# The pooling mixer's input product as sixteen pairs of seven products, its results through memory

## Chip, cores and metric

The kernel runs on one core of a Trainium2 chip. The metric is the device time of one execution in microseconds, taken as the median of several runs. The engines are named as in the profile: PE (matrix products; PEld loads its weights), DVE (elementwise, reads SBUF and the matmul results in PSUM), ACT (elementwise with a function table), POOL or Pool (elementwise, SBUF alone), SP (its queue issues all DMAs here).

## What is computed

Two transformer-like blocks over 1024 positions and 1024 channels. The first has a mixer (input product, a short and a long convolution, output product) and a gated FFN. The second begins with the pooling layer that the change is about, and ends with an attention layer:

```python
def pool_mixer(h, w_in, w_group, scale, w_out):
    u, z = jnp.split(h @ w_in, 2, axis=-1)            # 1024 -> 2 x 2048
    p = causal_multiscale_pool(u).reshape(B, S, 4, 512)
    y = jnp.einsum('bsgc,gcd->bsgd', p, w_group).reshape(B, S, 2048) * scale
    return (y * jax.nn.silu(z)) @ w_out               # 2048 -> 1024
# h = modulate(rmsnorm(x)); x = x + gate * pool_mixer(h, ...)
# pool: trailing mean over 2, 4, 8 or 16 positions (by channel group) minus u
```

The FFN of the first block is silu(conv3(h @ w_gate)) * (h @ w_up), then @ w_down. The shift, scale and gate vectors of the second block come from products of a small vector with large matrices, done on DVE.

## The kernel before

Activations lie with channels on the partitions: a tile is 128 channels by 512 positions, and positions come in two chunks, c = 0 and 1. Every fp32 operand is split in two parts, `hi` (rounded by ACT) and `lo` (the rest, a subtraction on Pool or DVE), and a product is three matmuls: hi.hi, hi.lo, lo.hi. Results are in eight PSUM banks.

The program is written in the order in which it is issued; each engine runs its own instructions in that order. Two devices interleave work: `chains`, generators of which `pump()` runs every one a step further, so that a number of `yield`s sets how many steps lie between its parts (`WAIT`, L30), and `bg`, a queue of small background jobs of which `pump(n)` runs n. Weights come in by `tick` (L245), which counts matmuls and starts DMAs and splits a fixed count ahead of their use.

An input product goes column by column: `mm_col` (L294) does 24 matmuls for 128 output channels and one chunk. For the FFN this is replaced by a Strassen-like scheme with seven products for eight: the two chunks and the two halves of the input channels are the blocks of the activations, a pair of 128-column units the blocks of the weights. `blocks_of_h` (L743) makes the activations' blocks, 11 and 21 of chunk 0 and then t2, t3, t4, t1, 22 of differences with chunk 1; class `Pair` (L819) makes the sums of weights s1 to s4 (`sums` L845, `added` L840), splits them (`keep` L832), runs a product of 12 matmuls (`product` L871, matmuls L882) and takes results from PSUM (`evac` L887). `steps` (L129) is the order: products 1 and 2 of the first six pairs, which need chunk 0 alone, then the rest of the first four, and from there on two pairs at a time, 14 products. `SUMS_AT` makes the first four pairs' sums on DVE in steps 1 to 4. Up to step 11 only chunk 0's blocks are needed; meanwhile `chain_ffn` (L795) makes chunk 1's norm and blocks. The FFN's results are stored to memory (`ff`) and loaded back for w_down.

The pooling layer before (L1345 on) uses `mm_col`: for each of four channel groups, four u units of two chunks, pooled by DVE (`pool_p` L1290: doublings of the window, L1298), interleaved with z units (`do_z`), the group product (`do_gm` L1323, matmuls L1333) and the output product of the units that are ready (`down`, matmuls L311). Its entry follows `chunk_out`, the last rows of w_down chunk by chunk: `evac_last_ffn` (L1211) adds into x and makes two sums of squares, `chain_pool` (L1246) makes the norm: column sums on DVE (`block_sums` L334), a small matmul (L347), a power on Pool (L389), a diagonal on DVE and ACT (`diag` L367), a spread by PE (L382, L383). u's first four units run over chunk 0 while chunk 1's norm is made. x is rescaled in bg (L1268).

## Time and profile before

| | us |
|---|---|
| median of 3 runs (2081.71 to 2082.65) | 2081.8 |
| the profiled execution | 2080.15 |
| its span, first to last instruction | 2078.4 |
| PE busy | 1995.9 |
| DVE busy | 1337.7 |
| POOL busy | 964.2 |
| ACT busy | 804.5 |

By the first matmuls of each part, the FFN's products run from 339.4 to about 801 us of the span, w_down to about 1053, the pooling layer's products from 1053.5 to about 1641, then attention. How to read the views: the timeline lists an engine's instructions with their start, duration, line of the code, and in brackets how long the engine sat idle before one and whose end released it. A matmul's duration in the timeline counts its overlap with the one before, so the distance of two starts is its price. Windows give each engine's busy time in a stretch, and PEclk, the share of PE's full clock that was granted. The chain of waits is followed back from the last instruction to what released each one.

### The profile page before, as it was taken

Reading aid. Unit: us, or ns where it says so; the run is one execution under the profiler, and the core shown is the slowest. Engines: PE = TensorE matmul, PEld = TensorE weight load, DVE = VectorE, ACT = ScalarE, POOL = GpSimd, SP = SyncE. Lnnn points to the kernel's source line nnn. Section 1 sums busy time; section 2 is a strip of 40 time slices with the busy share of each in tenths; the row PEclk is TensorE's granted clock in tenths of the full one; section 3 lists DMA queues with packets and bytes.
Section 4 is the critical chain, followed back from the end, with each engine's and each line's share of the span. In section 5 each row is a group of like instructions: output and inputs, shape, how many; then the busy total and the mean of one; then the engine's idle time right before and its main releaser. Section 6 shows DMA issues by size and latency. Waiting matters only on the chain.

```text
span 2078.4 us, 25796 instructions
## 1 busy us (share of the span) xinstructions
PE 1995.9 (96%) x9112; PEld 1655.3 (80%) x9112; DVE 1337.7 (64%) x2199; ACT 804.5 (39%) x1583; POOL 964.2 (46%) x816
## 2 busy tenths in 40 slices
...
GB/s 209 51 61 41 117 98 59 1 102 163 152 173 194 172 196 325 197 73 100 11 52 31 61 41 41 61 41 51 61 41 56 36 122 60 58 56 32 112 1 81
DMA packets 95969, 186.64 MB, mean 90 GB/s; under 512 B 10928, under 2 KB 17504, under 8 KB 95840
## 3 DMA queue, kind: packets, MB, share of 16 engines
...
## 4 chain that ended last, share of the span: by engine, by line
PE 80%; DVE 12%; issue 2%; DMA 2%; ACT 2%; POOL 1%; SPq 1%; DVEq 0%; ACTq 0%; POOLq 0%
PE p L302 34%; PE p L311 20%; PE p L882 15%; PE p L1333 4%; PE p L1827 2%; PE o L1632 1%; PE pT L1605 1%; DVE ws L842 1%; DVE cps L528 1%; DMA fl<-ff 1%; DVE c L916 1%; DMA adaw<-in_kv_ada_w 1%; DVE hu L1229 1%; PE sc L1552 1%; PE sc L1551 1%
## 5 line engine op out<-in xcount | busy, mean ns | idle before, releaser
L196 POOL TENSOR_TENSOR wlo<-raw,whi 128x512 fp32r<-128x512 f32 x260 | 350.3, 1368 | 327.2 <-ACT whi L195 157.5
L311 PE MATMUL p<-alo,whi 128*128 128x512 f32 x784 | 308.4, 393 | 7.0 <-POOL alo L421 7.0
L302 PE MATMUL p<-hhi,whi 128*128 128x512 f32 x784 | 308.5, 393 | 6.7 <-ACT hhi L414 6.7
L302 PE MATMUL p<-hlo,whi 128*128 128x512 f32 x784 | 307.7, 392 | 3.5 <-DVE hlo L415 3.5
L311 PE MATMUL p<-ahi,whi 128*128 128x512 f32 x784 | 309.1, 394 | 0.7 <-ACT yo L708 0.7
L311 PE MATMUL p<-ahi,wlo 128*128 128x512 f32 x784 | 308.0, 393 | 0.0
L302 PE MATMUL p<-hhi,wlo 128*128 128x512 f32 x784 | 307.1, 392 | 0.0
L882 PE MATMUL p<-hhi,whi 128*128 128x512 f32 x616 | 244.9, 398 | 15.5 <-DVE q L894 8.0
L882 PE MATMUL p<-hlo,whi 128*128 128x512 f32 x616 | 243.6, 395 | 0.0
L882 PE MATMUL p<-hhi,wlo 128*128 128x512 f32 x616 | 243.1, 395 | 0.4 <-POOL wlo L837 0.4
L195 ACT CAST whi<-raw 128x512 fp32r<-128x512 f32 x260 | 150.4, 618 | 239.9 <-PE p L311 149.1
L311 PEld LDWEIGHTS p<-alo,whi 128*128 128x128 f32 x784 | 149.1, 190 | 39.1 <-POOL alo L421 8.3
L302 PEld LDWEIGHTS p<-hhi,whi 128*128 128x128 f32 x784 | 148.7, 190 | 36.4 <-ACT hhi L414 6.7
L302 PEld LDWEIGHTS p<-hlo,whi 128*128 128x128 f32 x784 | 148.6, 190 | 34.8 <-DVE hlo L415 4.9
L311 PEld LDWEIGHTS p<-ahi,whi 128*128 128x128 f32 x784 | 148.9, 190 | 32.0 <-ACT yo L708 1.1
L311 PEld LDWEIGHTS p<-ahi,wlo 128*128 128x128 f32 x784 | 149.0, 190 | 31.4
L302 PEld LDWEIGHTS p<-hhi,wlo 128*128 128x128 f32 x784 | 148.3, 189 | 31.3 <-DVE wlo L196 0.2
L1343 DVE SCALAR_TENSOR_TENSOR x<-p,modv,x 128x512 f32<-128x512 f32 x128 | 95.7, 750 | 119.9 <-PE p L311 119.5
L528 DVE SCALAR_TENSOR_TENSOR cps<-u,vec,cps 128x1024 f32<-128x1024 f32 (+1 forms) x140 | 150.6, 1075 | 4.5
L882 PEld LDWEIGHTS p<-hhi,whi 128*128 128x128 f32 x616 | 117.9, 191 | 41.5 <-ACT c L914 8.4
L837 POOL TENSOR_TENSOR wlo<-ws,whi 128x512 fp32r<-128x512 f32 x66 | 96.7, 1471 | 92.7 <-ACT whi L834 80.2
L882 PEld LDWEIGHTS p<-hhi,wlo 128*128 128x128 f32 x616 | 118.0, 192 | 26.1 <-POOL wlo L837 0.8
...
## 6 DMA issues: line engine op xcount, KB each, us to landing
...
raw<-in_a_w_in SPq DMA_DIRECT2D x64, 256.0 KB, 3.0
raw<-in_w_gate SPq DMA_DIRECT2D x44, 256.0 KB, 5.0
raw<-in_w_up SPq DMA_DIRECT2D x44, 256.0 KB, 5.1
ff<-f SPq DMA_DIRECT2D x44, 256.0 KB, 4.8
raw<-in_w_down SPq DMA_DIRECT2D x44, 256.0 KB, 4.8
fl<-ff SPq DMA_DIRECT2D x44, 256.0 KB, 5.4
raw<-in_w_in SPq DMA_DIRECT2D x40, 256.0 KB, 3.1
```

The source lines that it names most:

```text
L195: (DVE.tensor_copy if on_dve else ACT.copy)(hi, t)
L196: (DVE if on_dve else POOL).tensor_tensor(lo, t, r32(hi), ALU.subtract)
L302: PE.matmul(ps, lhsT=wt[k // 4][:, sl], rhs=hh[k, c], start=(n == 0), stop=(n == 23))
L311: PE.matmul(ps, lhsT=wt[d // 4][:, sl], rhs=hh[c], start=(n == 0), stop=(n == last))
L528: DVE.scalar_tensor_tensor(dst[:, lo:hi], u[:, lo + k:hi + k], V("conv_b_w", k * 4 + j), src[:, lo:hi], ALU.mult, ALU.add)
L837: eng.tensor_tensor(lo, x, r32(hi), ALU.subtract)
L842: DVE.tensor_tensor(t, x, y, op)
L882: PE.matmul(ps, lhsT=wt[:, sl], rhs=hh, start=(begins and n == 0), stop=(n == 11), skip_group_check=True)
L916: bg.append(lambda k=k: DVE.scalar_tensor_tensor(y[:, 0:T], g[:, k:k + T], w(k), y[:, 0:T], ALU.mult, ALU.add))
L1333: PE.matmul(ps, lhsT=wt[k // 2][:, o:o + 128], rhs=hx[k, c], start=(n == 0), stop=(n == 11))
L1343: DVE.scalar_tensor_tensor(X[d, c], ps, modv[:, goff + d:goff + d + 1], X[d, c], ALU.mult, ALU.add)
L1827: PE.matmul(ps, lhsT=wt[d // 4][:, sl], rhs=hh[c][:, lo:hi], start=(n == 0), stop=(n == 11))
```

## The change

The pooling layer's input product takes the FFN's scheme. `plan` makes the order for any list of pairs; the FFN's is now gate and up pairs in turn, the pooling layer's sixteen pairs alternate u and z units (four groups' units in order). Class `Products` holds what was the FFN's loop. In both stages the first two pairs' sums of weights are made by DVE in the second chunk's rows of the product before (`lead`, one half of `sums` for each of four rows), and the next two pairs' by Pool in steps 1 and 3; in the first 12 steps every weight's low part is Pool's. `blocks_of_h` gets the shift vector, makes each operand a step before ACT casts it and issues DVE's low part a step later still.

In the pooling layer x is stored to `xp`, the pooled units to `pp` and silu(z) to `zz`, and they are loaded back: x and group 0 in the last ten steps, the other groups during the output product. The group product and the output product follow as a stage of their own. The diagonal of the second norm of each chunk (`d1`) is made after the blocks, and x is rescaled during the first group product. The taps of the FFN's convolution enter `bg` one after the other. The modulation's small matmul comes six yields after its sums instead of two. w_down's groups are 4, 4, 4, 4, 2, 4 units instead of 2, 4, 4, 4, 4, 4; its loads are cut two a step, and half of x is loaded later. The core of the diff:

```diff
-        "ffn0": (2, 1, 1), "ffn1": (4, 1, 2), "pool0": (2, 0, 1), "pool1": (4, 0, 2),
+        "ffn0": (2, 1, 1), "ffn1": (4, 1, 2), "pool0": (2, 1, 1), "pool1": (5, 2, 2),
...
+LEAD = (2, 4, 5, 6, 6, 6, 7, 8)
...
-    blocks = [[("w_gate", 0), ("w_gate", 2)], [("w_up", 0), ("w_gate", 4)]]
-    blocks += [[("w_up", f), ("w_gate", f + 4)] for f in range(2, NF - 4, 2)]
-    blocks.append([("w_up", NF - 4), ("w_up", NF - 2)])
-    pairs = [g for b in blocks for g in b]
...
+    def plan(pairs):
+        steps = [(g, 1) for g in pairs[:SIDE]] + [(g, 2) for g in pairs[:SIDE]]
+        steps += [(g, p) for p in (1, 2) for g in pairs[SIDE:EARLY]]
+
+        sums_at = {1: pairs[2], 3: pairs[3]}
+        steps += [(g, p) for p in (6, 7, 4, 5, 3) for g in pairs[:SIDE]]
+        for n in range(SIDE, len(pairs), 2):
+            for p in (1, 6, 2, 7, 5, 4, 3):
+                if n < EARLY and p in (1, 2):
+                    continue
+                steps += [(g, p) for g in pairs[n:n + 2]]
+        use = {}
+        for n, ((name, f), p) in enumerate(steps):
+            for u in ((f,) if p in (1, 2) else (f, f + 1)):
+                use.setdefault((name, u), 12 * n)
+        for n, (name, f) in [(0, g) for g in pairs[:2]] + list(sums_at.items()):
+            use[name, f + 1] = 12 * n
+        for name, f in sorted(use, key=lambda k: use[k]):
+            col(name, f)
+            stage_mm[name] = 12 * len(steps)
+        first_use.update(use)
+        return pairs, steps, sums_at
...
+    FFN = plan([(n, f) for f in range(0, NF, 2) for n in ("w_gate", "w_up")])
+    DOWN = ((0, 1, 2, 3), (4, 5, 6, 7), (8, 9, 10, 11), (12, 13, 14, 15), (16, 17), (18, 19, 20, 21))
...
+    POOLED = plan([("a_w_in_2", e) for f in range(0, 16, 2) for e in (f, 16 + f)])
...
+        queue = []
+
+        def cut(name, i, x, sh=None, on_pool=None):
+            hi = S("hhi", F32R)
+            if sh is None:
+                ACT.copy(hi, x)
+            elif on_pool:
+                y = S("hs")
+                ACT.activation(y, x, ACTF.Identity, bias=sh)
+                x, sh = y, None
+                ACT.copy(hi, x)
+            else:
+                ACT.activation(hi, x, ACTF.Identity, bias=sh)
+            if on_pool:
+                put_block(name, i, hi, x, sh, True)
+            else:
+                queue.append(lambda: put_block(name, i, hi, x, sh))
...
+        def later_on():
+            for _ in range(len(queue)):
+                queue.pop(0)()
+
+        sh = [shift and shift(k) for k in range(NK)]
         if c == 0:
             for k in range(NK):
                 hf[k] = get(k)
-                low("11" if k < 4 else "21", k % 4, hf[k], high(hf[k]), True)
+                later_on()
+                cut("11" if k < 4 else "21", k % 4, hf[k], sh[k], shift is None or k % 2)
                 if k % 2:
                     yield
+            later_on()
...
+        for name, make, shs in (("t2", make_t2, sh[4:]), ("t3", make_t3, d3), ("t4", make_t4, [None] * 4),
+                                ("t1", lambda i: t1[i], [None] * 4), ("22", lambda i: h2[i], sh[4:])):
             for i in range(4):
-                cut(name, i, ts[i])
+                t = make(i)
+                later_on()
                 yield
-        while due:
-            low(*due.pop())
+                cut(name, i, t, shs[i], i % 2)
+                yield
...
-            eng = DVE if small_op["n"] % 7 in SUB_DVE else POOL
+            eng = DVE if not small_op["early"] and small_op["n"] % 7 in SUB_DVE else POOL
...
-        def sums(self):
-            self.s1 = self.added(self.half(1, 0), self.half(1, 1), ALU.add)
-            self.s2 = self.added(self.s1, self.half(0, 0), ALU.subtract)
-            self.s3 = self.added(self.half(0, 0), self.half(1, 0), ALU.subtract)
-            self.s4 = self.added(self.half(0, 1), self.s2, ALU.subtract)
+        def sums(self, eng, n):
+            if n in (None, 0):
+                self.s1 = self.added(self.half(1, 0), self.half(1, 1), ALU.add, eng)
+                self.s2 = self.added(self.s1, self.half(0, 0), ALU.subtract, eng)
+            if n in (None, 1):
+                self.s3 = self.added(self.half(0, 0), self.half(1, 0), ALU.subtract, eng)
+                self.s4 = self.added(self.half(0, 1), self.s2, ALU.subtract, eng)
...
-        bg.append(lambda: ACT.activation(y[:, 0:T], g[:, 0:T], ACTF.Copy, scale=w(0)))
-        for k in (1, 2):
-            bg.append(lambda k=k: DVE.scalar_tensor_tensor(y[:, 0:T], g[:, k:k + T], w(k), y[:, 0:T],
-                                                           ALU.mult, ALU.add))
+
+        def scale():
+            ACT.activation(y[:, 0:T], g[:, 0:T], ACTF.Copy, scale=w(0))
+            for k in (1, 2):
+                bg.append(lambda k=k: tap(k))
+
+        def tap(k):
+            DVE.scalar_tensor_tensor(y[:, 0:T], g[:, k:k + T], w(k), y[:, 0:T], ALU.mult, ALU.add)
+            if k == 2:
+                bg.append(last)
...
+        def lead(self, d):
+
+            small_op["early"] = True
+            if d < 4:
+                self.group[self.pairs[d // 2]].sums(DVE, d % 2)
+            self.prep_to(LEAD[d])
+
+        def run(self, hook):
+            dma_ahead = clock["dma"]
+            clock["dma"] = FFN_DMA
+            for n, (g, p) in enumerate(self.steps):
+                self.prep_to(n + PREP_AHEAD + 1)
+                if n in self.sums_at:
+                    self.group[self.sums_at[n]].sums(POOL, None)
+                if n == 2 * EARLY:
+                    small_op["early"] = False
+                while len(stores) > 1:
+                    stores.popleft()()
+                self.group[g].product(p)
+                pump(2 if len(bg) > 4 else 1)
+                self.group[g].evac(p)
+                hook(n, len(self.steps) - n)
+            clock["dma"] = dma_ahead
...
-        yield
-        yield
+        for _ in range(6):
+            yield
...
-        if n == len(steps) - 10:
+        if left == 10:
             fl["load"], fl["cut"] = ff_load(DOWN[0])
             for f in fl["load"]:
                 f()
-        if n >= len(steps) - 7 and fl["cut"]:
-            fl["cut"].pop(0)()
-        if len(steps) - 8 <= n < len(steps):
-            load_xf(n - len(steps) + 8)
-    clock["dma"] = dma_ahead
+        if left <= 7:
+            for f in fl["cut"][:2]:
+                f()
+            del fl["cut"][:2]
+        if left <= 4:
+            load_xf(4 - left)
...
+        if n == 0:
+            todo = [lambda m=m: load_xf(m) for m in range(4, 8)] + todo
...
+    xp = dram.tile([D, T], F32, name="xp")
+    pp = dram.tile([2 * D, T], F32, name="pp")
+    zz = dram.tile([2 * D, T], F32, name="zz")
...
+        nc.sync.dma_start(out=rows_of(xp, d, c), in_=x)
+        if c == 1:
+            pooled.lead(d)
...
-        d1 = diag(r1)
         for _ in range(w1):
             yield
-        yield from make_h(c, spread(d2), 0, MOD_SH0, *SPREAD[f"pool{c}"])
+        ps = spread(d2)
+
+        def get(k):
+            h = S("h")
+            DVE.scalar_tensor_tensor(h, X[k, c], gain[:, k:k + 1], ps, ALU.mult, ALU.mult)
+            return h
+
+        def shift(k, n=1):
+            return modv[:, MOD_SH0 + k:MOD_SH0 + k + n]
+
+        yield from blocks_of_h(c, get, shift)
         yield
-        r1b = S("R1")
-        ACT.copy(r1b, spread(d1))
-        for k in range(NK):
-            def upd(k=k):
-                DVE.scalar_tensor_tensor(X[k, c], X[k, c], V("norm_final_g", k), r1b, ALU.mult, ALU.mult)
-            bg.append(upd)
+        d1 = diag(r1)
+        for _ in range(3):
+            yield
+        r1b[c] = S("R1")
+        ACT.copy(r1b[c], spread(d1))
...
+        gate_n["u", e] += 1
+        if gate_n["u", e] == 2:
+            pool_p(e)
...
+        def double(m):
+            n, s_ = L("ps"), h["s"]
+            if 2 * m < w:
+                POOL.memset(n[:, 0:16], 0.0)
+            DVE.tensor_tensor(n[:, 16:16 + T], s_[:, 16:16 + T], s_[:, 16 - m:16 - m + T], ALU.add)
+            h["s"] = n
+
+        def last():
+            s_ = h["s"]
+            f = small.tile([128, 16], F32, tag="fix", name="fix")
+            DVE.tensor_tensor(f[:, 0:w - 1], s_[:, 16:16 + w - 1], rcnt[:, 0:w - 1], ALU.mult)
+            DVE.tensor_tensor(f[:, 0:w - 1], f[:, 0:w - 1], u[:, 16:16 + w - 1], ALU.subtract)
+            DVE.scalar_tensor_tensor(s_[:, 16:16 + T], s_[:, 16:16 + T], 1.0 / w, u[:, 16:16 + T],
+                                     ALU.mult, ALU.subtract)
+            DVE.tensor_copy(s_[:, 16:16 + w - 1], f[:, 0:w - 1])
+            stores.append(lambda: nc.sync.dma_start(out=pp[e * 128:(e + 1) * 128, :],
+                                                    in_=s_[:, 16:16 + T]))
+
+        m = 1
+        while m < w:
+            bg.append(lambda m=m: double(m))
+            m *= 2
+        bg.append(last)
+
+    def put_z(i, c, ps, more):
+        t = S("sz")
+        if more is None:
+            ACT.activation(t, ps, ACTF.Silu)
+        else:
+            DVE.tensor_tensor(t, ps, more, ALU.add)
+            ACT.activation(t, t, ACTF.Silu)
+        stores.append(lambda: nc.sync.dma_start(out=rows_of(zz, i - 16, c), in_=t))
...
+        kc = [(k, c) for c in range(NC) for k in range(4)]
+        ic = [(i, c) for i in range(4 * g, 4 * g + 4) for c in range(NC)]
+        return ([lambda k=k, c=c: load(k, c) for k, c in kc] + [lambda i=i, c=c: load_z(i, c) for i, c in ic],
+                [lambda k=k, c=c: cut(k, c) for k, c in kc])
...
+                    for _ in range(min(4, len(todo))):
+                        todo.pop(0)()
...
+    def scale_x(d, c):
+        DVE.scalar_tensor_tensor(X[d, c], X[d, c], V("norm_final_g", d), r1b[c], ALU.mult, ALU.mult)
+
+    def in_pooled(n, left):
+        if left == 10:
+            nxt["load"], nxt["cut"] = load_group(0)
+        if 7 <= left <= 10:
+            for f in nxt["load"][:4]:
+                f()
+            del nxt["load"][:4]
+        if left <= 6:
+            for f in nxt["cut"][:2]:
+                f()
+            del nxt["cut"][:2]
+        if left <= 4:
+            load_xp(4 - left)
...
+    todo = []
+    for d in range(NK):
+        if d < 4:
+            todo.append(lambda d=d: load_xp(d + 4))
+        todo += [lambda d=d, c=c: scale_x(d, c) for c in range(NC)]
+    do_gm(0, todo)
+    for g in range(3):
+        todo = [f for part_ in load_group(g + 1) for f in part_]
+        out2(g, 0, todo, 2 if g == 2 else 1)
+        if g == 2:
+            do_gm(3, todo)
+        out2(g, 1, todo, 1)
+        if g < 2:
+            do_gm(g + 1, todo)
```

## Rows read from the trace of the kernel before

**Rows 1.** Head of the page, and engine shares of the span.

```profile
span 2078.4 us, 25796 instructions
...
PE 1995.9 (96%) x9112; PEld 1655.3 (80%) x9112; DVE 1337.7 (64%) x2199; ACT 804.5 (39%) x1583; POOL 964.2 (46%) x816
```

**Rows 2.** Chain that ended last, in order of time: start, us, what.

```profile
1189.83 54.40 PE p L302 x240
```

**Rows 3.** Timeline, PE, FFN: start, us, operation, [idle before <-releaser].

```profile
352.50 0.50 PE L382 MATMUL spread<-dh,ones 128*128 128x512 f32 x1 [3.08 <-DVE dh L376]
...
369.44 0.50 PE L882 MATMUL p<-hhi,wlo 128*128 128x512 f32 x1 [0.42 <-POOL wlo L837]
...
379.52 0.80 PE L882 MATMUL p<-hhi,whi 128*128 128x512 f32 x1 [7.52 <-ACT p L891]
...
455.84 0.77 PE L882 MATMUL p<-hhi,whi 128*128 128x512 f32 x1 [7.97 <-DVE q L894]
...
561.88 0.41 PE L347 MATMUL sums<-bsum,quad 128*128 128x32 f32 x2 [2.73 <-DVE bsum L340]
...
771.49 0.63 PE L347 MATMUL sums<-bsum,quad 128*128 128x32 f32 x2 [3.15 <-DVE bsum L340]
```

**Rows 4.** Windows: us, busy us (count) of each engine, PEclk, DMA share, GB/s.

```profile
379.60:385.20 5.60, 5.60 (x13) 4.38 (x14) 5.30 (x4) 2.73 (x6) 5.60 (x4) 0.50 0.00 0
...
566.00:767.00 201.00, 199.54 (x880) 164.32 (x879) 168.65 (x229) 72.38 (x114) 95.50 (x85) 1.00 0.74 181
...
1140.00:1625.00 485.00, 485.00 (x2141) 401.60 (x2140) 159.60 (x207) 110.81 (x195) 187.29 (x179) 1.00 0.16 51
```

**Rows 5.** Timeline, PE, entry of w_down.

```profile
825.09 0.50 PE L311 MATMUL p<-alo,whi 128*128 128x512 f32 x1 [1.53 <-POOL alo L421]
...
832.48 0.79 PE L311 MATMUL p<-alo,whi 128*128 128x512 f32 x1 [3.94 <-POOL alo L421]
```

**Rows 6.** Timeline, PE, entry of the pooling layer.

```profile
1038.45 0.50 PE L382 MATMUL spread<-dh,ones 128*128 128x512 f32 x1 [1.09 <-DVE dh L376]
...
1053.50 0.39 PE L302 MATMUL p<-hhi,whi 128*128 128x512 f32 x1
...
1057.73 0.50 PE L302 MATMUL p<-alo,whi 128*128 128x512 f32 x1 [1.12 <-POOL alo L421]
...
1067.87 0.41 PE L347 MATMUL sums<-bsum,quad 128*128 128x32 f32 x2 [0.57 <-DVE bsum L340]
```

**Rows 7.** Timeline, DVE, the same entry.

```profile
1067.13 0.69 DVE L340 TENSOR_REDUCE bsum<-tr 128x16 f32<-128x512 f32 x1
```

**Rows 8.** Lines of DVE from 1028 to 1068: count | busy, mean ns | idle.

```profile
L404 DVE TENSOR_TENSOR ssa<-ssa,sq 128x512 f32<-128x512 f32 x9 | 10.7, 1191 | 0.2
...
L376 DVE TENSOR_SCALAR dh<-ident,rh 128x128 fp32r<-128x128 f32 x8 | 1.7, 281 | 0.0
```

**Rows 9.** Lines of the whole run by form, same columns.

```profile
L842 DVE TENSOR_TENSOR ws<-raw 128x512 f32<-128x512 f32 x44 | 39.4, 894 | 0.0
...
L837 POOL TENSOR_TENSOR wlo<-ws,whi 128x512 fp32r<-128x512 f32 x66 | 96.7, 1471 | 92.7 <-ACT whi L834 80.2 <-issue 6.3 <-PE p L882 3.0
...
L1298 DVE TENSOR_TENSOR ps<-ps 128x1024 f32<-128x1024 f32 x24 | 29.4, 1226 | 7.0 <-POOL ps L1297 4.9
...
L1268 DVE SCALAR_TENSOR_TENSOR x<-x,vec,R 128x512 f32<-128x512 f32 x16 | 18.3, 1196 | 0.0
...
L1339 DVE SCALAR_TENSOR_TENSOR sz<-p,vec,sz 128x512 f32<-128x512 f32 x32 | 24.0, 751 | 149.8 <-PE p L1333 146.2 <-ACT sz L1312 2.3 <-ACT whi L195 1.4
```

**Rows 10.** Timeline, Pool, entry of the FFN.

```profile
318.58 1.30 POOL L837 TENSOR_TENSOR wlo<-raw,whi 128x512 fp32r<-128x512 f32 x1 [8.49 <-ACT whi L834]
...
348.81 1.51 POOL L389 TENSOR_TENSOR q<-r,neghalf 128x4 f32<-128x4 f32 x1 [3.14 <-DVE r L362]
```

**Rows 11.** Timeline, DVE, entry of the FFN.

```profile
319.06 1.36 DVE L837 TENSOR_TENSOR wlo<-raw,whi 128x512 fp32r<-128x512 f32 x1 [1.73 <-ACT whi L834]
```

**Rows 12.** Page, DMA issues: count, KB each, median us to landing.

```profile
fl<-ff SPq DMA_DIRECT2D x44, 256.0 KB, 5.4
```

311 lines of the change are left out of this document (118 added, 193 removed).

## Prediction, made before the change was run

> **What bounds the kernel now.** I read the page's head first [rows 1]: the profiled run took 2080.15 us, of which the span is 2078.4, and PE is busy for 96% of it; nothing else is near. Next the chain of waits, in order of time, over the pooling layer (from about 1100 to 1640 us): it names PE matmuls and nothing else, and one stretch gives the price of a matmul: 240 in 54.40 us, 0.2267 us each [rows 2]. The mean that the page gives for one matmul counts its overlap with the next, so it is not a price. The windows say the same: from 1140 to 1625 PE is busy for all of 485 us at clock 1.00 while DVE has 160 [rows 4]. There a matmul taken away is time taken away. Last I read PE's timeline for the places where it sat idle. They lie at the seams of stages and in the FFN, and each is followed back to its releaser [rows 3, 5, 6]. A long idle has a second price: in the window from 379.60 the granted clock is 0.50 and 13 matmuls take 5.60 us, 0.43 each, the lower of the two levels [rows 4]; that is 0.20 us lost on each, some 2.5 to 3 us after each of the longest waits.
>
> **A: the product itself.** Before, 32 units of 128 columns in 2 chunks of 24 matmuls are 1536. After, 16 pairs in 7 products of 12 are 1344. So 192 go, at 0.2267 us [rows 2]: **-43.5 us**. The other layers keep their counts.
>
> What the scheme asks of the other engines must hide beside PE. One block of two pairs is 14 products, 168 matmuls, 38.1 us. DVE then has 8 sums of weights at 0.89 (7.1), 4 low parts at about the same (3.6), 10 reads of PSUM at 0.75 (7.5), and for the widest window two units of four doublings at 1.23 and a last step that I price like one (12.3): 30.5 of 38.1 us. Pool has 10 low parts at 1.47, 14.7 us [rows 9]. If every DVE operation with two SBUF inputs took 1.19 us for 512 elements, the mean in the crowded seam [rows 8], DVE would need some 38 us in the two widest blocks and less in the rest. So the cover holds on average. Single pauses may show: **+2 us** (0 to +8). The FFN, the same scheme, has DVE busy 168.65 of 201 us and loses only 1.5 us of PE there, none of it to a product's operands [rows 4].
>
> **B: the way through memory.** Added are 16 stores and loads of x, 16 double-size stores and 32 loads of pooled units, 32 stores and loads of z. A load of this kind lands in 5.4 us [rows 12] and is issued seven steps or more (19 us) ahead of its use, so it is covered; the FFN sends its results through the same SP queue. The exit to the group product has one tight place: DVE still drains up to ten pooling steps (about 8 us), then has 16 rescalings of x at 1.20 in the first five of eight products [rows 9]. The fourth scaled product waits behind about 8 + 10.8 + 3.0 = 21.8 us of DVE, then a cast and Pool's low part, 2 us more; PE asks for it after 96 matmuls, 21.8 us. **+2 us** (0 to +8).
>
> **C: the FFN's entry.** PE waits 3.08 and 7.52 us there [rows 3], and with 0.42 for a low part, restarts and the half clock some 14.5 go. The first wait is for the second chunk's norm, queued on DVE among sixteen sums of weights; the second is an ACT copy, stuck behind casts that wait for DVE. Now eight sums (6 to 9 us of DVE) run in the rows of the preceding product, where two low parts of 1.36 and the waits of 1.73 before them go [rows 11], and two pairs' sums move to Pool. Pool pays about 1.3 us each, the price of its two-input step alone [rows 10]; four stand ahead of the power step that began at 348.81 [rows 10], behind them it begins at about 352. So the first wait stays: 5 us. The second mostly goes, since DVE loses 8 sums (6 to 7 us) and casts are issued a step later than their operands: 2 us left (0 to 7). **-7.5 us** (-2 to -11).
>
> **D: the FFN's middle.** At 455.84 PE had waited 7.97 us for DVE, which sat in the convolution of gate units, with 2.5 us of half clock behind it [rows 3]. Gate and up pairs now alternate, so the first four pairs bring four gate units instead of six (two taps less for each of two units, at the 1.23 of a step of that size [rows 9] 5 us), and a tap is queued only once its scaling is issued. **-8 us** (-3 to -10.5). The modulation vectors' small matmuls make PE wait five times, from 3.15 us down to 0.21, 7.3 in all (the first and the last stand in [rows 3]); with restarts and half clock 12.5. They now come six pumps, three products or 8 us, after their sums instead of one. The last one, after the last rows of w_down, may cost its 3 us again. **-9.5 us** (-5 to -12).
>
> **E: the entry of w_down.** Three waits for Pool's low part, 1.53, one like it, and 3.94 us [rows 5], with half clock 9.2. The first group now has four units instead of two, and its loads are split two per step before the FFN ends. **-8.5 us** (-4 to -9).
>
> **F: the pooling layer's entry, where the time is given back.** Before, PE waits 1.09, 1.12 and one like it, and 0.57 us [rows 6]: 3.9 in all. Three things change. DVE gets 8 sums more in the second chunk's rows, at 0.89 (7.1); it loses one low part (1.19), a diagonal (four steps of 0.28, 1.1) and waits that the later issue avoids (about 3, the spread's 1.09 and two of ACT's casts) [rows 6, 8, 9], so its last reduction, which ends at 1067.8 [rows 7], ends about 1.8 later, at 1069.6. Next, the diagonal of the first chunk's second norm, which was made early, now stands behind that reduction on DVE: its spread is ready 1.1 us later, at about 1070.7. And PE meets this spread after 24 matmuls of the new stage, where the old stage had 48 before it needed DVE's end: the products begin at 1053.5 [rows 6], with 1.5 us for the first spread and 24 x 0.2267 that is 1060.4. PE then waits **10.3 us** (5 to 17), with 2.9 of half clock. The first spread waits 2.5 instead of 1.09 (eight Pool steps share the queue with its power step), and the products that need the second chunk lose about 1 (0 to 5). Sum against before: 10.3 + 2.9 + 1.4 + 1.0 - 0.6 = **+15 us** (+4 to +24). Behind the waiting spread on PE stand all later products; ACT's copies wait with them.
>
> **The sum.** -43.5 + 2 + 2 - 7.5 - 8 - 9.5 - 8.5 + 15 = **-58 us**. From 2080.15 that is 2022; the median of the runs lies 1.65 above the profiled one, so **2024 us**.
>
> **The rivals.** *The entry is absorbed.* F lies at its lower end, because Pool leaves DVE its short times and PE comes later: 11 less, 2013 us. For it: DVE's sums take 0.69 when Pool is idle. Against: Pool is full in those rows. 15%.
>
> *Pool's sums hold up DVE.* Beside Pool's low part from 318.58 to 319.88, a DVE step that began at 319.06 took 1.36 us, ending 0.54 after Pool's [rows 10, 11]: the shorter price of such a step, counted from Pool's end. If each of the eight Pool sums of an entry (10.4 us) blocks DVE's differences in this way, the second chunk is late by most of that: C loses its 7.5 and F grows by 6, 2037 us. It decides if the sums still run when the spread is done; by C's count four of eight do. [...] 15%.
>
> *The FFN's waits only move.* DVE is 84% busy in the FFN; with PE earlier, C, D and E bring 10 instead of 33.5: 2047 us. For it: the same engines must do the same work in less time. Against: PE's waits there come singly, between them it had none. 10%.
>
> *Slower.* The SP queue issues in order. 80 stores and 80 loads are new, and a store that waits for ACT or DVE holds the weight halves behind it. If PE loses 1.6 us for each of the 80 stores (128 us in all), the gain of 58 becomes a loss of 70: 2152 us. The point from which it decides is 58/80 = 0.7 us for each store. Against it speaks that the FFN's 44 stores cost PE nothing that the timeline shows. 5%.
>
> *Nothing changes*, because PE was not what ended last: 2081 us, 2%; the chain of rows 2 speaks against it.
>
> **How the numbers follow.** The forecast has the remaining 53%. Its own bounds, with half of them met at a time, give 2010 to 2040. To leave out no more than 2 in 10 the range takes in the absorbed entry and the lock, and part of the moved waits: 2006 to 2048. About 0.2% (4 us) is what a measurement of this kernel can tell from no change. Faster: 53 + 15 + 15 + 10 = 93%; same 2%; slower 5%.
>
> **What the profile after would show.** PE has 192 matmuls fewer, 8920. Within the new products PE is busy without gaps at 0.2267 us; if not, A's cover was wrong. At the layer's entry one PE wait of about 10 us for a spread, released by DVE or ACT, and the half clock behind it. No wait over 1 us for the modulation sums in the FFN, none for Pool's low parts at w_down; a first FFN wait of about 5 us, now after Pool. [...] The prediction is wrong if PE waits inside the products, for slots, stores or DVE.

## The result, and the profile after

| | before | after |
|---|---|---|
| median, us | 2081.75 | 2067.11 |
| profiled run, span, us | 2080.15, 2078.4 | 2067.11, 2065.3 |
| PE matmuls | 9112 | 8920 |
| DVE busy, us | 1337.7 | 1499.9 |

The ratio of after to before is 0.9933, with a 95% interval of 0.9916 to 0.9951: faster by 14.6 us, where 58 were forecast and 2048 was the upper end of the range. So the sign was right and the size was wrong by 43 us. The head of the page of after:

```profile
span 2065.3 us, 26176 instructions
...
PE 1961.7 (95%) x8920; PEld 1623.9 (79%) x8920; DVE 1499.9 (73%) x2365; ACT 841.3 (41%) x1647; POOL 1042.2 (50%) x871
```

The 192 matmuls are gone, as step A said, and they were worth their price: in this window of after (columns as in [rows 4]), in the middle of the new products, PE is busy all the time, and 309 matmuls begin (the count of 311 takes in two that began before it): 0.2265 us each.

```profile
1230.00:1300.00 70.00, 70.00 (x311) 57.96 (x310) 48.56 (x61) 22.29 (x40) 28.13 (x29) 1.00 0.33 110
```

To see where the rest went I measure the **loss** of a stretch: its length on PE's timeline less 0.2267 us [rows 2] for each matmul of 512 columns in it. It holds waits, small matmuls and half clock together.

| stretch (us from the start, before; after) | loss before | loss after | change | forecast |
|---|---|---|---|---|
| FFN, entry (339.4 to 420; 337.5 to 420) | 15.4 | 15.4 | 0.0 | C -7.5 |
| FFN, 420 to 475 | 10.5 | 2.9 | -7.6 | D -8 |
| FFN, rest (475 to 800.7; 475 to 787.8) | 16.1 | 12.6 | -3.5 | D -9.5, with the next but one |
| w_down, entry (800.7 to 870; 787.8 to 860) | 9.8 | 0.3 | -9.5 | E -8.5 |
| w_down, middle (to 1010) | 0.2 | 7.2 | +7.0 | in D |
| seam to the pooling layer (1010 to 1110; 1010 to 1120) | 7.2 | 29.6 | +22.4 | F +15 |
| within the products (to 1640; to 1382.3) | -0.1 | 11.6 | +11.7 | A +2 |
| exit to the group product (after: 1382.3 to 1440) | in the line above | 13.6 | +13.6 | B +2 |
| seam to the attention layer | 6.6 | 8.1 | +1.5 | 0 |

With the 43.5 us of A and 5.1 us in the first mixer and behind the pooling layer, which the change does not touch (in the runs below the same code scatters by 4 us in each of these two parts, so that these 5.1 us may be scatter), the lines give the 13.1 us by which the span is shorter, to 0.1. The first line is good to 2 us: in five runs whose edits lie elsewhere the FFN's first wait is 4.7 us and not 6.27. The waits behind the losses, on PE's timeline of after (start, us, operation, idle time before it and its releaser):

```profile
349.40 0.61 PE L346 MATMUL sums<-bsum,quad 128*128 128x16 f32 x2 [6.27 <-DVE bsum L339]
360.43 0.50 PE L381 MATMUL spread<-dh,ones 128*128 128x512 f32 x1 [3.75 <-DVE dh L375]
448.73 0.47 PE L902 MATMUL p<-hhi,whi 128*128 128x512 f32 x1 [2.67 <-DVE q L914]
...
677.68 0.64 PE L346 MATMUL sums<-bsum,quad 128*128 128x32 f32 x2 [4.01 <-DVE bsum L339]
...
769.10 0.50 PE L902 MATMUL p<-hhi,wlo 128*128 128x512 f32 x1 [1.86 <-POOL wlo L855]
...
988.37 0.64 PE L346 MATMUL sums<-bsum,quad 128*128 128x32 f32 x2 [4.01 <-DVE bsum L339]
...
1061.47 0.80 PE L381 MATMUL spread<-dh,ones 128*128 128x512 f32 x1 [15.72 <-DVE dh L375]
1089.94 0.80 PE L902 MATMUL p<-hhi,whi 128*128 128x512 f32 x1 [3.57 <-ACT p L911]
1164.90 0.77 PE L902 MATMUL p<-hhi,whi 128*128 128x512 f32 x1 [6.16 <-DVE q L914]
...
1388.94 0.49 PE L1428 MATMUL p<-ahi,whi 128*128 128x512 f32 x1 [2.35 <-ACT ahi L419]
...
1416.68 0.80 PE L310 MATMUL p<-alo,whi 128*128 128x512 f32 x1 [1.29 <-POOL alo L420]
```

The FFN's two entry waits of [rows 3] (3.08 and 7.52) have turned into two others of about the same size; its wait of 7.97 is 2.67; the waits of [rows 5] at w_down's entry are gone; the entry of the pooling layer, 1.12 and 0.57 in [rows 6], now waits 15.72 and 3.57; and there are four new places: in the FFN at 769, where Pool makes low parts of w_down's weights before this one, in w_down at 988, in the products at 1165, and at the exit from 1389 on. Behind most of them the granted clock is 0.50, the lower of the two levels in [rows 4]; behind those of 2.67 and 1.86 us it is 1.00. The windows behind the waits at 1164.90 and 1388.94:

```profile
1165.00:1168.00 3.00, 3.00 (x7) 2.36 (x8) 2.09 (x2) 0.00 (x0) 1.54 (x2) 0.50 0.86 268
...
1391.00:1396.00 5.00, 5.00 (x13) 3.75 (x12) 4.42 (x5) 0.00 (x0) 4.10 (x7) 0.50 0.00 0
```

One more view of after, DVE and then Pool at the two entries, is what the first theory comes from. The diagonal of a scale (four steps, line 375) takes 3.94 and 3.93 us where Pool makes its first sums (line 860) beside it, and 0.87 where Pool does not:

```profile
356.44 3.94 DVE L375 TENSOR_SCALAR dh<-ident,rh 128x128 fp32r<-128x128 f32 x4
...
1057.48 3.93 DVE L375 TENSOR_SCALAR dh<-ident,rh 128x128 fp32r<-128x128 f32 x4
...
1068.39 0.87 DVE L375 TENSOR_SCALAR dh<-ident,rh 128x128 fp32r<-128x128 f32 x4
...
358.83 1.25 POOL L860 TENSOR_TENSOR ws<-raw,ws 128x512 f32<-128x512 f32 x1
...
1059.88 1.26 POOL L860 TENSOR_TENSOR ws<-raw,ws 128x512 f32<-128x512 f32 x1
```

The slow diagonals end 0.30 and 0.27 us after the last of these sums (360.38 after 360.08, 1061.41 after 1061.14). In the FFN Pool's sums do a second thing. The diagonal's chain goes through a power step on Pool, and four sums stand ahead of it there, so that it starts at 354.02 and DVE stands idle:

```profile
355.07 1.25 DVE L371 CAST rh<-q 128x4 fp32r<-128x4 f32 x1 [4.35 <-POOL q L388]
```

### The profile page after: what moved, and what is told of

Read it like the earlier page. It is cut to its first block, busy times and chain, and to the rows that moved or that the text cites. A ratio compares the mean times of both kernels' runs of the same rounds, so it can differ in the third digit from the quotient of the medians.

```text
span 2065.3 us, 26176 instructions
## 1 busy us (share of the span) xinstructions
PE 1961.7 (95%) x8920; PEld 1623.9 (79%) x8920; DVE 1499.9 (73%) x2365; ACT 841.3 (41%) x1647; POOL 1042.2 (50%) x871
## 3 DMA queue, kind: packets, MB, share of 16 engines
q8 instruction: 70, 1.15, 0.2%
## 5 line engine op out<-in xcount | busy, mean ns | idle before, releaser
L902 PE MATMUL p<-hhi,whi 128*128 128x512 f32 x1064 | 421.2, 396 | 12.5 <-DVE q L914 8.8
L902 PE MATMUL p<-hhi,wlo 128*128 128x512 f32 x1064 | 419.4, 394 | 3.4 <-POOL wlo L855 3.2
L902 PE MATMUL p<-hlo,whi 128*128 128x512 f32 x1064 | 419.3, 394 | 0.7 <-POOL hlo L735 0.7
L195 POOL TENSOR_TENSOR wlo<-raw,whi 128x512 fp32r<-128x512 f32 x196 | 261.8, 1359 | 144.3 <-ACT whi L194 91.0
L855 POOL TENSOR_TENSOR wlo<-ws,whi 128x512 fp32r<-128x512 f32 x116 | 168.1, 1453 | 251.6 <-ACT whi L852 208.9
L902 PEld LDWEIGHTS p<-hhi,whi 128*128 128x128 f32 x1064 | 203.1, 191 | 58.4 <-ACT whi L852 10.4
L902 PEld LDWEIGHTS p<-hhi,wlo 128*128 128x128 f32 x1064 | 202.9, 191 | 48.2 <-POOL wlo L855 4.5
L902 PEld LDWEIGHTS p<-hlo,whi 128*128 128x128 f32 x1064 | 202.9, 191 | 43.5 <-POOL hlo L735 1.1
L301 PE MATMUL p<-hhi,whi 128*128 128x512 f32 x496 | 196.1, 395 | 6.7 <-ACT hhi L413 6.7
L301 PE MATMUL p<-hlo,whi 128*128 128x512 f32 x496 | 195.4, 394 | 3.5 <-DVE hlo L414 3.5
L301 PE MATMUL p<-hhi,wlo 128*128 128x512 f32 x496 | 194.7, 393 | 0.0
L852 ACT CAST whi<-ws 128x512 fp32r<-128x512 f32 x152 | 92.6, 620 | 240.2 <-DVE ws L860 225.1
L855 POOL TENSOR_TENSOR wlo<-raw,whi 128x512 fp32r<-128x512 f32 x84 | 120.3, 1437 | 98.4 <-ACT whi L852 86.7
L194 ACT CAST whi<-raw 128x512 fp32r<-128x512 f32 x196 | 112.1, 617 | 92.9 <-PE p L310 77.6
```

The costliest lines, as they stand in the source:

```text
L194: (DVE.tensor_copy if on_dve else ACT.copy)(hi, t)
L195: (DVE if on_dve else POOL).tensor_tensor(lo, t, r32(hi), ALU.subtract)
L301: PE.matmul(ps, lhsT=wt[k // 4][:, sl], rhs=hh[k, c], start=(n == 0), stop=(n == 23))
L852: ACT.copy(hi, x)
L855: eng.tensor_tensor(lo, x, r32(hi), ALU.subtract)
L902: PE.matmul(ps, lhsT=wt[:, sl], rhs=hh, start=(begins and n == 0), stop=(n == 11), skip_group_check=True)
```

## The experiments

Each run was timed beside runs of the kernel before, so I compare ratios to before. The kernel after stands at 0.9933; 0.0010 of ratio is 2.1 us. Each edit is one on the kernel after. Steps of the products are counted from 0, by PE's matmuls. Three theories were set against one another for the two entries: **Pool beside DVE** (Pool's sums stretch DVE's steps; the second rival of the prediction), **tail** (DVE comes late out of the last rows because of the sums made there) and **order** (the spread of chunk 0's second scale stands too early for PE).

**late_pool_sums.** Pool's sums go to later steps.

```
-        sums_at = {1: pairs[2], 3: pairs[3]}
+        sums_at = {7: pairs[2], 9: pairs[3]}
```

> Edit: Pool makes the first sums of the third and fourth pair at steps 7 and 9 of each product run instead of 1 and 3, in both runs (FFN and pooling mixer). Theory 'Pool beside DVE' (Pool's sums stretch the DVE steps that build the diagonals): the four 128x128 steps of a diagonal fall from 3.9 to about 0.9 us at both entries; the FFN's wait of 3.75 us for the diagonal falls under 1, the pooling entry's wait of 15.72 falls by 4 to 5 to about 11; in all 6 to 9 us less than the kernel after: 2058 to 2061. Theory 'order' (the spread of chunk 0's second scale stands too early in TensorE's order) and theory 'tail' (DVE comes too late out of the last rows, because of the sums made in them): the diagonal's four steps may get shorter, but the pooling entry still waits 14 us or more; 2064 to 2068.

2068.13 us, 0.9950 (0.9934 to 0.9967). The waits did what the first theory said: the FFN's 3.75 is gone and 15.72 is 11.73. The time did not. In the FFN 5 us came back 22 us further on, as a wait for ScalarE's copy, in the pooling run 2.3 at step 34 (8.48 for 6.16). The new wait in the FFN, the smaller one at the pooling entry, and what ScalarE stood idle for ahead of that copy, a low part that comes behind four of the moved sums in Pool's order:

```profile
382.04 0.79 PE L902 MATMUL p<-hhi,whi 128*128 128x512 f32 x1 [5.04 <-ACT p L911]
...
1058.04 0.80 PE L381 MATMUL spread<-dh,ones 128*128 128x512 f32 x1 [11.73 <-DVE dh L375]
...
380.88 0.62 ACT L749 CAST hhi<-t 128x512 fp32r<-128x512 f32 x1 [6.43 <-POOL wlo L855]
```

So the stretching is real (4.0 us of the 15.72), but moving Pool's sums only moves what they hold up.

**late_d1.** The diagonal of chunk 0's second scale is made 29 pauses later.

```
-        yield
+        for _ in range(1 if c else 30):
+            yield
         d1 = diag(r1)
```

> Edit: the diagonal of chunk 0's second scale (the one that rescales the residual stream) is made 29 pauses later, some 15 steps into the products. Theory 'order' (this spread alone holds TensorE): the wait of 15.72 us at the pooling entry falls under 4; 2053 to 2056. Theory 'tail' (DVE comes too late out of the last rows; the spread is only the first that meets it): TensorE goes on for some 6 matmuls and then waits 8 to 10 us at the next small matmul, the sums over chunk 1, which needs DVE's reduction that ended at 1056.3; 5 to 7 us less than after: 2060 to 2062. Theory 'Pool beside DVE': as 'tail', but the wait is 5 to 6 and what ends it is a step that Pool's sums hold up; the FFN's waits are as they were in all three.

2060.78 us, 0.9911 (0.9897 to 0.9926), and the wait is the one that "tail" named, at the size it named:

```profile
1056.65 0.64 PE L346 MATMUL sums<-bsum,quad 128*128 128x32 f32 x2 [9.29 <-DVE bsum L339]
```

The place of this spread costs 6.4 us of the 15.72; behind it stands DVE's last reduction, whatever comes first on PE.

**no_row_sums.** The first two pairs' sums are not made in the rows, but when their step is prepared.

```
-            if d < 4:
-                self.group[self.pairs[d // 2]].sums(DVE, d % 2)
```

> Edit: the first sums of the first two pairs are not made on DVE within the rows of the product before, but by DVE when their step is prepared (steps 8 and 9 and later), in both runs. Theory 'tail': DVE leaves the rows 5 to 8 us earlier; the FFN's first wait of 6.27 us falls to 0 to 2, the pooling entry's 15.72 to 8 to 10; 2053 to 2058. Theory 'order' and theory 'Pool beside DVE': the FFN's first wait stays over 4 us, the pooling entry's over 13; and DVE, with these sums beside the blocks of chunk 1, makes a new wait of 2 to 6 us at steps 10 to 16; 2066 to 2073.

2069.61 us, 0.9954 (0.9939 to 0.9969): no gain. The FFN's wait for the reduction is gone, and the next link of the same chain takes its place, DVE's wait for the power step behind Pool's sums:

```profile
356.16 0.80 PE L381 MATMUL spread<-dh,ones 128*128 128x512 f32 x1 [8.89 <-DVE dh L375]
...
350.83 1.23 DVE L371 CAST rh<-q 128x4 fp32r<-128x4 f32 x1 [7.07 <-POOL q L388]
```

The pooling entry's 15.72 fell only to 14.44. "Tail" in its simple form falls: the sums in the rows make the reduction late, but with Pool's sums ahead of the power step and beside the diagonal, PE gains nothing from that.

**lead_sums_dve.** The sums that the change gave to Pool go back to DVE, at the same steps.

```
-                    self.group[self.sums_at[n]].sums(POOL, None)
+                    self.group[self.sums_at[n]].sums(DVE, None)
```

> Undoes one part of the change: the first sums of the third and fourth pair are made by VectorE, not GpSimd, at the same steps 1 and 3, in both runs. Theory 'Pool beside DVE': the diagonals fall to 0.9 us and VectorE has 8 steps of 0.68 more: the FFN's wait of 3.75 stays at 3 to 5, the pooling entry's 15.72 at 14 to 17; 2065 to 2069, no loss. Rival 'VectorE's queue' (its own length is all that counts): 5.5 us more of VectorE's work ahead of the diagonal and of chunk 1's blocks in each run: the waits of the two entries grow by 4 to 6 each; 2073 to 2079.

2057.35 us, 0.9890 (0.9873 to 0.9908), a clear gain that neither theory forecast: 16 more steps on DVE make the kernel faster by 9 us. DVE's busy time on the page is 1502.2 us instead of 1499.9, 2.3 more for 16 steps that take 0.69 each, so the other steps became shorter by some 9. The diagonal, with Pool idle, and one of the four sums behind it:

```profile
351.57 0.87 DVE L375 TENSOR_SCALAR dh<-ident,rh 128x128 fp32r<-128x128 f32 x4
352.35 0.69 DVE L860 TENSOR_TENSOR ws<-raw 128x512 f32<-128x512 f32 x1
```

The FFN's wait for the diagonal is gone (a copy now waits 2.14), and the loss of its entry falls from 15.4 to 12.5. At the pooling entry 15.72 falls to 11.69. There the power step isn't behind Pool's sums, so these 4 us are the stretching alone; in the FFN stretching and Pool's order went together.

**undo_first_sums.** All four pairs' first sums on DVE at steps 1 to 4, none in the rows, as in the kernel before.

```
-        sums_at = {1: pairs[2], 3: pairs[3]}
+        sums_at = {n + 1: pairs[n] for n in range(4)}
...
-            if d < 4:
-                self.group[self.pairs[d // 2]].sums(DVE, d % 2)
...
-                    self.group[self.sums_at[n]].sums(POOL, None)
+                    self.group[self.sums_at[n]].sums(DVE, None)
```

> Undoes the second half of the change: the first sums of the four leading pairs are made by VectorE alone at steps 1, 2, 3 and 4 of each run, as in the kernel before; none in the rows of the preceding product and none on GpSimd. Theory 'early sums are worth what the prediction said': the FFN's entry loses the 7.5 us that step C counted, with a wait of 7 us for ScalarE's copy as in [rows 3], and the pooling entry, whose rows get lighter, gets back about as much: 2072 to 2078 if the pooling entry gets back little, 2066 to 2069 if as much. Rival 'Pool beside DVE' (GpSimd's sums cost more than they save): the FFN is at most 3 us longer, the pooling entry's wait of 15.72 falls to 8 or less and its wait of 3.57 for ScalarE's copy rises by 3 to 6; 2058 to 2064, faster than the kernel after.

2055.48 us, 0.9883 (0.9868 to 0.9898): the second half of the change, undone, gives back 10 us, of which the run before, with Pool's sums alone undone, had 9. The FFN got shorter, not longer (446.0 us from its first product to w_down's first row, 450.3 in after), the pooling run too (339.2, 343.2). The rival's sign holds; its wait of 8 or less came out as 10.61. The FFN's first wait is 4.09 us here, with eight of DVE's own sums ahead of the diagonal.

**side_sums_pool.** The opposite: Pool makes the fifth and sixth pair's sums as well.

```
-        sums_at = {1: pairs[2], 3: pairs[3]}
+        sums_at = {1: pairs[2], 3: pairs[3], 22: pairs[4], 24: pairs[5]}
```

> Edit: the first sums of the fifth and sixth pair too are made by GpSimd, at steps 22 and 24, in both runs: 8 steps of 0.68 us less on VectorE in each, 8 of 1.26 more on GpSimd, which stands idle for 6 us twice between 1142 and 1157. Theory 'VectorE's queue' (the wait of 6.16 us for q at 1164.9 is the length of VectorE's queue since 1142): the wait falls under 2 us, the one of 2.67 in the FFN goes; 6 to 10 us less than after with the half clock behind: 2057 to 2061. Rival 'Pool beside DVE' (each of GpSimd's sums holds VectorE up for about its own length): VectorE's steps between 1130 and 1165 grow by as much as they become fewer, the wait stays at 5 to 8; 2066 to 2070.

2081.43 us, 1.0010 (1.0001 to 1.0020): slower than after by 16 us, worse than either theory, and DVE has fewer steps. DVE itself now sits idle, for Pool's four sums in a row and for a cast behind them:

```profile
423.35 1.77 DVE L735 TENSOR_TENSOR hlo<-h,hhi 128x512 fp32r<-128x512 f32 x1 [5.97 <-POOL ws L860]
...
434.14 1.11 DVE L855 TENSOR_TENSOR wlo<-ws,whi 128x512 fp32r<-128x512 f32 x1 [7.02 <-ACT whi L852]
```

No stretching shows in the sum here: DVE's busy time on the page falls by 10.8 us (1489.1 for 1499.9), as much as 16 steps of 0.68 come to, so the rival's mechanism fails in this run. What costs is Pool's own order, a queue of 5 us for a set of four (1.29 each), behind which low parts wait, and DVE and PE with them. Pool's sums thus have two prices: at the entries they stretch DVE's steps (four of the diagonal from 0.87 to 3.94 us), and they hold up what stands behind them on Pool (5 us for a set of four).

**ada12 and ada2.** The pauses between a modulation section's reduction and its small matmul, 12 instead of 6 (shown), or 2.

```
-        for _ in range(6):
+        for _ in range(12):
             yield
```

> Edit: 12 pauses instead of 6 between a modulation section's reduction and its small matmul. Theory (the matmul stands too early behind a DVE whose queue is long): the two waits of 4.01 us (at 677.68 and 988.37) and the half clock behind them go; 8 to 13 us less than after: 2054 to 2059. Rival (DVE's queue is what is long, so that a later matmul only moves the wait to the next evacuation that DVE owes): 2 us or more of each wait come back as waits for q or for an evacuation within 15 us; 2063 to 2068.

2074.37 us, 0.9978 (0.9968 to 0.9987). The wait at 677 goes, the FFN as a whole keeps its 450.4 us (450.3 in after; a copy now waits 3.35), and the one in w_down grows from 4.01 to 14.83:

```profile
997.16 0.64 PE L346 MATMUL sums<-bsum,quad 128*128 128x32 f32 x2 [14.83 <-DVE bsum L339]
...
984.99 8.00 DVE L1093 SCALAR_TENSOR_TENSOR ada<-adaw,cact,ada 128x512 f32<-128x512 f32 x12
```

The DVE row tells why. Twelve steps of the last section run one behind the other, with no row's addition between them: the rows are over, and the chain, longer by 48 pauses, is run out by the loop that drains it while PE has nothing. The wait at 988.37 in after is the same thing with 32 pauses more than before.

> Undoes one part of the change: 2 pauses instead of 6 between a modulation section's reduction and its small matmul, so that the chain of eight sections is 32 pauses shorter. Theory of step D (each small matmul came too early): the FFN gets waits of 3 to 0.2 us at four or five of them back, 6 to 10 us with the half clock, while the wait of 4.01 at the end of w_down (the chain's remainder, run out with no rows between) goes, 4 to 6 us: 2067 to 2073. Rival 'waits only move in the FFN' (more pauses won nothing there): the FFN stays within 2 us of 450, w_down loses 4 to 6: 2060 to 2064.

2085.39 us, 1.0031 (1.0019 to 1.0044), against both: w_down is 7 us shorter, but the FFN is 476.4 us long, 26 more. Six waits for these matmuls, from 0.86 to 7.92 us and 23.4 together, stand where the kernel before had 7.3 with the same two pauses; the third and the last:

```profile
613.06 0.64 PE L346 MATMUL sums<-bsum,quad 128*128 128x32 f32 x2 [4.91 <-DVE bsum L339]
...
783.62 0.64 PE L346 MATMUL sums<-bsum,quad 128*128 128x32 f32 x2 [7.92 <-DVE bsum L339]
```

So the four pauses are worth 20 us in this kernel, and something else in the change had made the waits of the two-pause order three times as long. The change's other edits of the FFN (order of the pairs, queue of the taps) were not undone alone, so which of them it was stays open.

**bg_slow and hold_run_sums.** Both aim at the 6.16 us for q at step 34 (37 in two of the expectations). The first (first diff) issues fewer queued steps, the second queues the first tiles' running sums later.

```
-                pump(2 if len(bg) > 4 else 1)
+                pump(1)
```

```
+    held = []
...
         if gate_n["u", e] == 2:
-            pool_p(e)
+            held.append(e)
...
     def in_pooled(n, left):
+        if held and 36 <= n < 45 and n % 2 == 0:
+            pool_p(held.pop(0))
+        while held and n >= 45:
+            pool_p(held.pop(0))
```

> Edit: of the queued steps of VectorE (taps of the convolution, doublings and corrections of the running sums) one is issued after each product instead of two while more than four are queued; the one issued within a product stays. Theory 'VectorE's queue' (1024-wide steps issued two at a time stand ahead of the reads of PSUM): the pooling run's wait of 6.16 us for q goes under 3 and the FFN's 2.67 under 1, with the half clock behind: 5 to 9 us less, 2058 to 2062, unless more steps are left for the end of the run: then the exit waits grow by 3 to 8 and it is 2062 to 2068. Rival: the wait for q is made by the sums and low parts of the weights, not by the queued steps: it stays over 5; 2066 to 2069.

2067.61 us, 0.9942 (0.9927 to 0.9956): nothing; the wait stays 6.16. Alone this would have spoken for the rival.

> Edit: the running sums of the pooling mixer's first tiles are not queued when their tile is done (steps 27 to 31) but one at a time at steps 36 to 44, and from step 45 as before. Theory 'running sums in VectorE's queue': TensorE's wait of 6.16 us for q at 1164.9 and the half clock behind it go, at most 2 us come back in the 20 steps behind: 5 to 9 us less than after, 2058 to 2062. Rival (the wait is made by the reads of PSUM, the sums and the low parts of the weights of steps 28 to 37): the wait stays over 4 us: 2065 to 2069.

2059.05 us, 0.9901 (0.9886 to 0.9915). The wait is gone; 0.87 and 0.71 come back behind it, and the loss from about 1120 to 1215 falls from 9.2 to 2.1. So it was the running sums, by where they fall, not by how many are issued at a time. A stretch of 23 us over the same products, first in after, then here:

```profile
1142.00:1165.00 23.00, 16.84 (x75) 13.64 (x73) 21.34 (x30) 6.40 (x11) 8.15 (x6) 0.98 0.29 104
```

```profile
1136.00:1159.00 23.00, 23.00 (x103) 19.05 (x102) 12.06 (x17) 7.74 (x14) 9.47 (x7) 1.00 0.40 138
```

DVE (fourth figure) is busy 21.34 us of 23 where PE waits, and 12.06 where it does not.

**memset_dve, no_rescale and exit_low_dve.** They take the exit apart. In after, two doublings of the last running sums wait for a zeroing of 16 columns that Pool has queued behind low parts (for the first, Pool's rows are shown):

```profile
1385.89 1.23 DVE L1361 TENSOR_TENSOR ps<-ps 128x1024 f32<-128x1024 f32 x1 [8.72 <-POOL ps L1360]
...
1391.55 2.28 DVE L1361 TENSOR_TENSOR ps<-ps 128x1024 f32<-128x1024 f32 x1 [2.70 <-POOL ps L1360]
...
1383.27 2.54 POOL L420 TENSOR_TENSOR alo<-pl,ahi 128x512 fp32r<-128x512 f32 x2
1385.75 0.15 POOL L1360 MEMSET ps<- 128x16 f32 x2
```

memset_dve puts the zeroing on DVE; no_rescale leaves the rescalings out altogether; exit_low_dve is memset_dve with the first group's low parts on DVE. The three diffs in this order:

```
-            POOL.memset(t[:, 0:16], 0.0)
+            DVE.memset(t[:, 0:16], 0.0)
...
-                POOL.memset(n[:, 0:16], 0.0)
+                DVE.memset(n[:, 0:16], 0.0)
```

```
-        todo += [lambda d=d, c=c: scale_x(d, c) for c in range(NC)]
```

```
-            PP_H[g, k, c], PP_L[g, k, c] = split(tiles.pop((k, c)))
+            PP_H[g, k, c], PP_L[g, k, c] = split(tiles.pop((k, c)), DVE if g == 0 else None)
```

> Edit: the zeroing of the 16 leading columns of a running sum (the pooling mixer's u tiles and its doublings) is done by VectorE itself instead of GpSimd. Theory 'zeroing queued on Pool' (a doubling on VectorE waits for a zeroing that stands in GpSimd's order behind the low parts of the group's operands): VectorE's idle times of 8.72 and 2.70 us at 1385.89 and 1391.55 go, the gate results of the last pairs reach ScalarE some 10 us earlier, and TensorE's waits from 1389 to 1425 (2.35, 0.85, 1.29, 0.44, 1.29, 1.19, with half clock behind two of them) shrink to under 2 us in all; 9 to 14 us less than the kernel after: 2053 to 2058. Rival 'rescaling' (the 16 rescalings of the residual stream between VectorE's scalings of the group product are what makes the rows late): the idle times go, but the waits at 1413 to 1424 and their half clock stay; 3 to 5 less: 2062 to 2064.

2061.85 us, 0.9914 (0.9894 to 0.9934). DVE's idle times and the waits from 1411 to 1425 go, but the loss of the exit only falls from 13.6 to 10.5: PE now waits 3.19, 1.33, 0.57 and 0.56 us for Pool's low parts. The time is near the rival's, the waits are neither theory's. Both engines' steps are longer where they run side by side. DVE, then Pool:

```profile
1387.08 2.17 DVE L1361 TENSOR_TENSOR ps<-ps 128x1024 f32<-128x1024 f32 x1
...
1383.55 9.04 POOL L420 TENSOR_TENSOR alo<-pl,ahi 128x512 fp32r<-128x512 f32 x4
```

A doubling takes 2.17 us, 1.23 in the row of after above; a low part 2.26 (9.04 for four), 1.27 there.

> Leaves out: the 16 steps that rescale the residual stream by the second norm's scale within the first group product (the loads of the second half of that stream stay). Theory 'zeroing queued on Pool': the waits at 1388.9 and 1390.3 (2.35, 0.85, with half clock behind) stay as they are, and of those from 1413 to 1424 at least half; 2 to 5 us less than after: 2062 to 2065. Rival 'rescaling': the waits at 1413 to 1424 and their half clock go; 6 to 8 less: 2059 to 2061.

2057.30 us, 0.9888 (0.9870 to 0.9906): the rival's waits went, as it said, and the first two stayed; the loss of the exit is 5.9. The 7.7 us of loss between this run and after are the rescalings' price here: 16 on DVE, between the gates that the output product waits for. This price and the 3.1 us of the zeroing were each measured with the other left in; that they add up is not shown.

> Two edits: the zeroing on VectorE as in the run memset_dve, and the eight low parts of the first group's operands on VectorE instead of GpSimd. [...] Rival 'VectorE's queue' (8 more steps on the fuller engine): the group product waits for VectorE's scaled gates instead, 4 us or more at 1390 to 1420: 2062 to 2067.

2064.87 us, 0.9922 (0.9903 to 0.9941), in the rival's range. Within the group product no wait is left in its 96 matmuls (21.6 us). But DVE comes to the rescalings 19.1 us after the group product's start (22.1 in after), and PE waits for the gates among them, 3.27, 1.00, 0.73 and 1.02 us; the loss of the exit stays 10.5. Either place is paid as long as the rescalings stand where they are.

**combo1, combo2, combo3.** The repairs together. combo1: lead_sums_dve, late_d1, memset_dve, two instead of four of the queued steps after each product of the first group, and 3 instead of 4 pauses between the steps of the last two modulation sections. combo2: the same with undo_first_sums for lead_sums_dve. combo3: combo2 with hold_run_sums and exit_low_dve. The two edits not yet shown:

```
-                    for _ in range(min(4, len(todo))):
+                    for _ in range(min(2 if g == 0 else 4, len(todo))):
...
-        todo = [f for part_ in load_group(g + 1) for f in part_]
+        todo += [f for part_ in load_group(g + 1) for f in part_]
...
-            for _ in range(ADA_GAP):
+            for _ in range(ADA_GAP if i < 6 else 3):
```

> Five edits on the kernel after: all first sums on VectorE (as in the run lead_sums_dve), the diagonal of chunk 0's second scale 29 pauses later (late_d1), the zeroing on VectorE (memset_dve), two instead of four of the queued loads and rescalings of the residual stream after each product of the first group, the last four behind it, and 3 instead of 4 pauses between the modulation steps of the last two sections. Theory (each wait has a cause of its own): 10 + 6 + 5 + 5 + 4 = 30 us less than after: 2034 to 2040. Rival 'waits only move' (VectorE's queue meets TensorE at the next place): half of that, 2048 to 2055.

2044.34 us, 0.9823 (0.9804 to 0.9842): 23 us less than after, between the two.

> Five edits on the kernel after: all first sums of the leading pairs by VectorE at steps 1 to 4 (as in the run undo_first_sums), the diagonal of chunk 0's second scale 29 pauses later, the zeroing on VectorE, the rescalings two a product, 3 pauses for 4 in the last two modulation sections. Theory (separate causes): 11.6 + 6.3 + 5.3 + 3 + 6 = 32 less than after: 2033 to 2039. Rival 'handed on' (the second chunk's chain on VectorE is what TensorE meets whatever is moved ahead of it): as the run combo1, 2042 to 2047.

2045.03 us, 0.9835 (0.9819 to 0.9851): the rival's size. The sums' gain and the late diagonal's don't add: behind the first product of the pooling layer PE's waits come to 20.0 us in after, 13.9 in late_d1, 15.9 in undo_first_sums, and still 14.8 here; w_down has no wait any more (242.6 us, 251.3 in after).

> The five edits of combo2, with the running sums of the first tiles one at a time from step 36 on (hold_run_sums) and the first group's low parts on VectorE (exit_low_dve). Theory (separate causes): of combo2's waits, 6.16 at step 37 and 5.66 for low parts in the first group product, each with 2 to 3 us of half clock, go, 2 come back elsewhere: 14 less than combo2's 2045: 2030 to 2034. Rival 'handed on': VectorE, with eight low parts more and the running sums later, is late for the gates or for q behind step 44: 2040 to 2045.

2036.13 us, 0.9792 (0.9778 to 0.9805): faster than before by 43 us and than after by 29, so the best of all here. The running sums and the exit are repaired (the loss from 1100 to 1200 is 1.9, that of the exit 8.1). What is left is the pooling layer's entry:

```profile
1040.32 0.64 PE L346 MATMUL sums<-bsum,quad 128*128 128x32 f32 x2 [8.19 <-DVE bsum L339]
...
1071.67 0.80 PE L902 MATMUL p<-hhi,whi 128*128 128x512 f32 x1 [5.21 <-ACT p L911]
```

Its loss, over 81 us from the first product on, is still 21.2 us (25.5 in after, 4.6 before) with every cause removed that the runs name. Whatever is taken out of DVE's way ahead of the second chunk, PE meets the next link of that chunk's chain.

## Why the prediction was right or wrong

The span was to fall by 58 us and fell by 13.1. The terms that missed are D (13.4 us, 13.0 of them in the modulation's matmuls), B (11.6), the pauses in A (9.7), C (7.5) and F (7.4); E, the seam to the attention layer and the untouched parts together gave 4.6 of this back.

**A, the product.** -43.5 was right, matmul for matmul. Its second term, pauses of +2 within the products, was +11.7. The step that failed is the cover by averages: 30.5 us of DVE's work in a block of 38.1. The running sums of the first four tiles fall together between 1136 and 1162 us, and in the 23 us up to the end of the wait at step 34 DVE is busy for 21.34; hold_run_sums took 7.1 of the 11.7 away. The prediction's own worse case would not have covered even the average: at 1.19 us for 512 elements its ten steps of 1024 elements take 2.38 each, and the block comes to 45.6 us, not to "some 38". The prediction's own sign of failure ("if PE waits inside the products, for slots, stores or DVE") is what happened.

**B, the way through memory.** +2 was +13.6. The stores and loads cost nothing that the timeline shows: among all that PE waited for in after there is no DMA. The 21.8 us of DVE against 21.8 of PE were the tight place, as written, but ahead of it DVE stood idle for 11.4 us, because two of its steps waited for a zeroing in Pool's order. The step that failed is that sum of DVE's work, which held no wait for Pool, although [rows 9] has 4.9 us of DVE's idle time ended by this zeroing (line 1297). Of the 13.6 the rescalings left out bring 7.7 and the zeroing moved brings 3.1; no run explains the rest.

**C, the FFN's entry.** -7.5 was 0.0. The first wait was forecast at 5 and is 6.27; the wait for ScalarE's copy is gone, as said; but 3.75 us for the diagonal are new. The step that failed priced Pool's sums at "the price of its two-input step alone" and at nothing for DVE. The queue ahead of the power step had been counted (a start at about 352, measured 354.02), the 3.94 us for the diagonal had not. The first wait of 6.27 is for the reduction, which the sums in the rows make late, and not for Pool (it is gone in no_row_sums). Undoing the early sums brings 4 of the 7.5 us; for the rest no run has a cause.

**D, the FFN's middle.** The wait for q: -8 forecast, -7.6 measured, by the convolution's order. The modulation's matmuls: -9.5 forecast, +3.5 measured (-3.5 in the FFN, where the new wait of 1.86 for Pool at 769 is counted in, +7.0 in w_down). The mechanism was right and worth more than forecast, 20 us by ada2. Two things were missed. The same pauses make the chain 32 longer, so that its last section runs out behind the rows: the prediction gave this 3 us as a possibility, and it took 7. And with two pauses this kernel would wait 23 us there, not the 7.3 of before, so that a row of before was no measure of what the pauses had to cover.

**E, the entry of w_down.** -8.5 forecast, -9.5 measured, all three waits gone. No run undoes a part of this edit alone; the splits that now come before the FFN ends stand ahead of the low part that PE waits 1.86 us for at 769.

**F, the pooling layer's entry.** +15 forecast, +22.4 measured. The order of events was right: PE reaches the spread of chunk 0's second scale early and waits for DVE. PE was there 6.6 us after the first product (6.9 forecast), DVE's last reduction ended 17.2 us after it (16.1 forecast); the diagonal then took 5.1 us with its cast instead of 1.1, 4.0 of it Pool beside it (lead_sums_dve). With the reduction 1.1 us later than forecast that is 5.4 of the missing 7.4; the rest is the copy's wait of 3.57 with its half clock, forecast at 1. F's sum also left the two waits of about 1.1 us of [rows 6] out; they are gone, and one of 0.71 stands in their place.

**The rivals.** "Pool's sums hold up DVE" (15%) had its two figures nearly right, C losing its 7.5 and F growing by 7.4 where it said 6. For C that is in part luck: undoing Pool's sums brings back 2.9 of the 7.5 (lead_sums_dve). Its time, 2037, was still 30 off, since B, the pauses and the modulation missed by 34 us beside it; that Pool's sums hold DVE's steps up is shown by lead_sums_dve and undo_first_sums. The forecast's range names a lock, and no run shows one; what the runs show is steps that take longer side by side, the four of the diagonal 3.94 us beside Pool's sums in after and 0.87 in lead_sums_dve with Pool idle. side_sums_pool shows another thing, what waits in Pool's order. "The FFN's waits only move" held for the modulation's pauses beyond six (ada12) and not for the convolution or w_down's entry. Its sum was near even so: C, D and E brought 13.6 us, where it said 10 and the forecast 33.5. The SP queue as the cause of a loss did not appear (the new stores are 64 by the prediction's own list, not 80). F stayed within its own bounds; A's pauses, B, C and D's modulation ended beyond theirs. A's pauses, F and what the runs explain of B and C come from a fuller DVE and Pool, and so fell on the same side, while the range met half of the bounds at a time; D's part in w_down is a count of pauses and has nothing to do with it.
